# A hybrid RWKV-7 and pooling layer on one core: the stream's low weight parts on GpSimd, earlier loads for the output projection, no root in the key's norm, and a reordered tail

## The chip, the core and the metric

The kernel runs on one core of a Trainium2 chip. A core has a matrix engine (TensorE, PE in the profile, with PEld for its weight loads), three engines for elementwise work (VectorE = DVE, ScalarE = ACT, GpSimd = POOL), a queue engine (SyncE = SP) and DMA queues that the engines issue to. Each engine works through its own instructions in order, and waits where an instruction needs what another engine or a DMA has not delivered. The metric is the time of one execution in microseconds (us).

## What is computed

One layer for 512 tokens of width 2048. The essential lines of the reference:

```python
h = rms_norm(x, norm_g[i])
z = jnp.einsum('btd,dn->btn', h, w_in[i])
...
kk = (k * k_k[i]).astype(f32).reshape(B, T, N_HEADS, HEAD_SIZE)
kk = kk / jnp.maximum(jnp.linalg.norm(kk, axis=-1, keepdims=True), KK_EPS)
k = k * (1.0 + (a - 1.0) * k_a[i])
...
y = wkv7_scan(rh, wh, kh, vh, kk, ah)
y = head_group_norm(y, ln_w[i], ln_b[i])
...
y_mix = jnp.concatenate([y_rwkv, y_pool], axis=-1)
x = x + jnp.einsum('btc,cd->btd', y_mix, w_out[i])
gate = jax.nn.sigmoid(jnp.einsum('btd,de->bte', x, w_pg[i]) + b_pg[i])
x = x + gate * jnp.einsum('btq,qd->btd', p[i], w_ple[i])
...
return rms_norm(x, final_g)
```

z is cut into the key, receptance, value and gate of 16 heads of 64 (k, r, v, g) and into the inputs and gates of a pooling branch. `wkv7_scan` is a recurrence over the tokens, with a 64x64 state per head that each token decays, corrects along kk and adds to.

## The kernel before

All large products are made in three matmuls per tile (`mm3`): each operand is split into a high part in the matrix engine's rounded format and a low part, the rest; high·high, high·low and low·high are summed. A weight chunk is fetched and split by `wsplit` (L127): SP loads it into `raw`, ScalarE casts it to `whi` (L132), VectorE subtracts to `wlo` (L133). Activations are split the same way by `split` (L137, L138).

The program has these stages.

1. The input norm, transposes and small parameters, to about 40 us. `prm` holds the parameter vectors, one column per 128 channels (`pc`), and `dprm` the columns derived from them (`dp`).
2. The **stream**, to 746 us. TensorE's order is written out (`keep_in_program_order` while `pin` is set). A generator `stream()` makes the projections: for each of 8 head pairs j the units k, r, v and g; 16 units of the pooling branch (b) spread among them; and at the end four embed units (e) that compute p @ W_ple, store the result `ple` to DRAM (`pled`), and use two PSUM tiles in turn (`psA`). `pump(n)` lets the stream issue n matmuls. `chunk` (L174) takes the next weight chunk and fetches up to two ahead; raw, whi and wlo have four buffers each.
   Among the stream's matmuls stand the steps of the recurrence. The 512 tokens are cut into chunks of 64, and `recur` makes for each a chain of three **hops**: `py` (TensorE) to `zs` (VectorE, L753); `pu` to `uv` (ScalarE, L761); `ps` to the new state `sbd` (VectorE, L772), from which GpSimd makes the decayed `s0p` (L779) for the next chunk. Behind each hop stand stream matmuls (`pump(HC1)` and its like), so that TensorE has work while the hop runs. In the same time VectorE carries out the next head pair's `invert`: 31 steps of two small instructions each (L624, L628), placed three steps at a time behind a hop's VectorE instruction.
   Between two head pairs stand `prepare_key`, `norm_key` and `scale_key` (L521 to L541): the square of k·k_k, its sum over a head on TensorE (`pss`), the root on ScalarE (L535), a maximum on VectorE (L536), the reciprocal (L540) and the product kk. The maximum is kept as `late[0]`: `gather` issues its two transposes y (L701), from which TensorE makes `pq`, only behind it, and `scale_key` behind the second of them.
3. The output projection (`acc_o`), to 935 us, in four blocks of 512 columns. The layer's input to it lies in DRAM (`yd`); 16 loads `yin` (L890, three buffers) are issued on ScalarE's queue and split into `yhi` and `ylo`, in the order 8 to 13, 0 to 7, 14, 15.
4. The gate projection (`acc_g`), to 1112.7 us, in four blocks; the last one finishes one tile of 128 tokens after the other, the last of these in two halves (`acc_h`).
5. The **tail**. `gate` (L987) makes tanh of the gate, the sum with the residual and its square with a running sum (`ssq`); in the last block GpSimd multiplies by the final gain gB into `x3` (L1007). `norm` (L1011) makes one over the root of the mean: for the first three token tiles by a bit trick and three Newton steps on VectorE (`rsqrt`, L141), for the last by ScalarE's Sqrt and a reciprocal. Then four pieces of 512 columns are scaled and written out by SP (L1034).

What sets the order: inside the stream the matrix engine's is fixed by hand; on the other engines a scheduler places each instruction by priority, unless `issue_after` ties it behind another.

Of the kernel before, what the change touches and what calls it, by code (L numbers as in the profile page):

```python
# [9 lines left out]
F32 = mybir.dt.float32  # L10
# [24 lines left out]
def trunk_kernel(ctx: ExitStack, tc: tile.TileContext, x, p, norm_g, w_in, mu, w0, w_up, a0, a_up,  # L35
# [79 lines left out]
    dprm = cst.tile([P, 25 + 8 * 8], F32, name="dprm")  # L115

    def pc(n_, i):
        return prm[:, col[n_] + i:col[n_] + i + 1]
# [1 line left out]
    def dp(o, i):  # L120
        return dprm[:, o + i:o + i + 1]
# [2 lines left out]
    hlo = hp.tile([P, KT, T], F32R, name="hlo", tag="alo")  # L124


    def wsplit(src, kt, n, nm):  # L127
        raw = wp.tile([P, kt, n], F32, name=f"raw_{nm}", tag="raw")
        nc.sync.dma_start(out=raw, in_=src)
        hi = wp.tile([P, kt, n], F32R, name=f"whi_{nm}", tag="whi")  # L130
        lo = wp.tile([P, kt, n], F32R, name=f"wlo_{nm}", tag="wlo")
        nc.scalar.copy(hi, raw)  # L132
        nc.vector.tensor_tensor(lo, raw, hi.bitcast(F32), ALU.subtract)  # L133
        return hi, lo

    def split(hi, lo, src):
        nc.scalar.copy(hi, src)  # L137
        nc.vector.tensor_tensor(lo, src, hi.bitcast(F32), ALU.subtract)  # L138
# [176 lines left out]
    def derived(o, n_, cnt, m_, a_):  # L315
        nc.vector.tensor_scalar(dprm[:, o:o + cnt], prm[:, col[n_]:col[n_] + cnt], m_, a_, ALU.mult, ALU.add)
# [113 lines left out]
    def embed_unit(ec):  # L430
        ws = [chunk(f"e{ec}_{k}", 0) for k in range(2)]
        phi, plo = phl
        for tt in range(NT):
            ts_ = slice(tt * P, (tt + 1) * P)
            pq = psA.tile([P, EC], F32, name=f"pple{ec}_{tt}", tag="acc")
            for k in range(2):
                wh, wl = ws[k]
                mm(pq, phi[:, k, ts_], wh[:, 0, :], start=k == 0, stop=False)
                mm(pq, phi[:, k, ts_], wl[:, 0, :], start=False, stop=False)
                mm(pq, plo[:, k, ts_], wh[:, 0, :], start=False, stop=k == 1)  # L440
                if k == 0:
                    yield 3
            t_ = pp.tile([P, EC], F32, name=f"ple{ec}_{tt}", tag=("u", "sw")[tt % 2])
            nc.scalar.copy(t_, pq)
            nc.scalar.dma_start(out=pled[ts_, ec * EC:(ec + 1) * EC], in_=t_)
            yield 3
# [83 lines left out]
    def norm_key(j):  # L530
        kk, kqh, kql = kks[j]
        ps = psM.tile([P, T], F32, name=f"pss{j}", tag="m")
        mm(ps, blk, kqh, start=True, stop=False)
        mm(ps, blk, kql, start=False, stop=True)
        nc.scalar.activation(kk, ps, AF.Sqrt)  # L535
        late[0] = nc.vector.tensor_scalar(kk, kk, 1e-12, None, ALU.max)  # L536

    def scale_key(j):
        k_, kk = need("k", j), kks[j][0]
# [5 lines left out]
    def prepare(j):  # L545
# [332 lines left out]
    s2a.close()  # L878
    psB = ctx.enter_context(tc.tile_pool(name="psB", bufs=3, space=PSUM))
    lp = ctx.enter_context(tc.tile_pool(name="lp", bufs=1))  # L880
    pump(10 ** 6)
    pin[0] = False
    sy = ctx.enter_context(ExitStack())
    ymp = sy.enter_context(tc.tile_pool(name="ymp", bufs=1))
    yhi = ymp.tile([P, KT, T], F32R, name="yhi")
    ylo = ymp.tile([P, KT, T], F32R, name="ylo")
    order = [8, 9, 10, 11, 12, 13, 0, 1, 2, 3, 4, 5, 6, 7, 14, 15]
    for k in order:
        t_ = ymp.tile([P, T], F32, name=f"yin{k}", tag="yin", bufs=3)
        nc.scalar.dma_start(out=t_, in_=yd[k])  # L890
        split(yhi[:, k, :], ylo[:, k, :], t_)


    x2hi = hp.tile([P, KT, T], F32R, name="x2hi", tag="ahi")
# [1 line left out]
    x2d = dram.tile([T, D], F32, name="x2d", bufs=1)  # L896
    KEEP = 8
    TP = 40
    AS = (3,)
    last = [None]  # L900
    nacc = [0]

    def acc_tile(nm):
# [71 lines left out]
    with tc.tile_pool(name="fp", bufs=2) as fp, tc.tile_pool(name="kp_", bufs=1) as kp_:  # L975
# [5 lines left out]
        def vectors(ec):  # L981
# [4 lines left out]
            nc.scalar.dma_start(out=gB, in_=final_g[es].unsqueeze(0).to_broadcast([P, EC]))  # L986
            return bB, gB  # L987

        def gate(acc, ec, tt, cs, part):
# [9 lines left out]
            nc.vector.tensor_tensor(gt, acc, bB[:, lc], ALU.add)  # L999
            nc.scalar.activation(gt, gt, AF.Tanh, scale=0.5)  # L1000
            if part > LAST:
                tc.keep_in_program_order(nc.scalar.activation(warm, epsr, AF.Sqrt))
            nc.vector.scalar_tensor_tensor(gt, gt, 1.0, pl_[:, lc], ALU.add, ALU.mult)  # L1003
            nc.vector.scalar_tensor_tensor(gt, gt, 0.5, x2_[:, lc], ALU.mult, ALU.add)  # L1004
            nc.scalar.activation(x2_[:, lc], gt, AF.Square, accum_out=ssq[tt][:, part:part + 1])  # L1005
            if part <= LAST:
                (nc.gpsimd if ec == LAST else nc.vector).tensor_tensor(x3[tt][:, cs], gt, gB[:, lc], ALU.mult)  # L1007
            return gt

        def norm(tt, parts):  # L1010
            rows = slice(tt * P, (tt + 1) * P)  # L1011
            rs = fp.tile([P, 1], F32, name=f"frs{tt}", tag="frs")
            nc.vector.tensor_reduce(rs, ssq[tt][:, 0:parts], mybir.AxisListType.X, ALU.add)
            nc.vector.tensor_scalar(rs, rs, 1.0 / D, 1e-6, ALU.mult, ALU.add)
            if tt < NT - 1:
                fr = fp.tile([P, 1], F32, name=f"fr{tt}", tag="fr")
                ft = fp.tile([P, 1], F32, name=f"ft{tt}", tag="ft")
                rsqrt(fr, rs, ft)
                rs = fr
            else:  # L1020
                nc.scalar.activation(rs, rs, AF.Sqrt)
                nc.vector.reciprocal(rs, rs)
            for pc_ in range(D // EC):
                ps_ = slice(pc_ * EC, (pc_ + 1) * EC)
                if tt == NT - 1 and pc_ == LAST:
                    hs = slice(pc_ * EC, pc_ * EC + EC // 2)
                    nc.scalar.activation(x3[tt][:, hs], x3[tt][:, hs], AF.Copy, scale=rs)
                    nc.vector.scalar_tensor_tensor(x3[tt][:, hs.stop:D], last[0], rs, vec[1][:, EC // 2:EC],
                                                   ALU.mult, ALU.mult)
                elif pc_ in ((1,) if tt == NT - 1 else AS):  # L1030
                    nc.scalar.activation(x3[tt][:, ps_], x3[tt][:, ps_], AF.Copy, scale=rs)
# [22 lines left out]
        for tt in range(NT):  # L1054
            fetch(ec, tt)
        acc = proj(w_pg, x2hi, x2lo, ec, "g", keep=kept)
        for tt in range(NT):
            ts_ = slice(tt * P, (tt + 1) * P)
            hw = EC // len(acc[tt])
            for h, a_ in enumerate(acc[tt]):  # L1060
                hc = slice(h * hw, h * hw + hw)
                for k in range(KT - KEEP, KT):
                    wh, wl = kept[k]
                    mm3(a_, x2hi[:, k, ts_], x2lo[:, k, ts_], wh[:, 0, hc], wl[:, 0, hc], False, k == KT - 1)
                with tc.high_priority(offset=TP * tt):
                    last[0] = gate(a_, ec, tt, slice(ec * EC + hc.start, ec * EC + hc.stop), ec + h)
            with tc.high_priority(offset=TP * tt):
                norm(tt, LAST + len(acc[tt]))


_INS = ["x", "p", "norm_g", "w_in", "mu", "w0", "w_up", "a0", "a_up", "k_k", "k_a", "r_k", "ln_w", "ln_b",
# [19 lines left out]
```

## Time and profile before

| | us |
|---|---|
| three runs | 1126.79, 1126.81, 1129.08; median 1126.81 |
| profiled execution | 1126.0 |
| its span on the core | 1124.3 |

The span lies 1.7 us under the execution's own time. The busy time of the engines by stage (windows view; columns: from and to, length, then busy time and number of instructions of PE, PEld, DVE, ACT, POOL, then the granted clock, the DMA share and GB/s):

```profile
40.00:160.00 120.00, 119.91 (x685) 98.51 (x684) 85.49 (x201) 55.41 (x102) 4.13 (x9) 1.00 0.38 105
160.00:720.00 560.00, 546.01 (x3471) 439.44 (x3470) 420.38 (x1273) 244.16 (x513) 53.41 (x106) 1.00 0.34 92
720.00:746.40 26.40, 25.37 (x109) 19.39 (x107) 9.37 (x19) 14.90 (x25) 0.00 (x0) 1.00 0.75 239
746.40:935.00 188.60, 182.30 (x816) 150.53 (x816) 70.21 (x107) 55.92 (x94) 0.00 (x0) 0.98 0.48 161
935.00:1112.70 177.70, 177.69 (x835) 148.20 (x833) 87.34 (x157) 60.10 (x113) 3.88 (x3) 1.00 0.49 157
1112.70:1124.30 11.60, 0.00 (x0) 0.00 (x0) 5.75 (x20) 4.75 (x11) 0.73 (x1) 0.68 0.51 181
```

TensorE works for 546.0 of 560 us of the stream's main part; a busy matmul is pipelined, so this is not a measure of its peak. Between 720 and 746.4 lie the embed units, and the last row is the tail, in which TensorE has nothing left to do.

### The profile page before, as it was taken

The numbers are of one execution on the slowest core, as the hardware profiler recorded it, in microseconds if no ns is written. First come the engines' busy times: TensorE is split into PE (matmuls) and PEld (weight loads), VectorE is DVE, ScalarE is ACT, GpSimd is POOL, SyncE is SP. The second block draws the span as 40 slices with busy tenths as digits, with TensorE's granted clock in tenths as the row PEclk, the third lists the DMA queues.
The fourth block names the chain that finished last, engine by engine and source line by source line (L and its number), as shares of the span: only waits on it lengthen the run. The fifth ranks groups of instructions, "written<-read, shape, count | busy, mean of one in ns | idle before, by whom it ended". The sixth has DMA issues, their size and how long they took to land. (4 is left out here: it accounts for less than half of the span.)

```text
span 1124.3 us, 17316 instructions
## 1 busy us (share of the span) xinstructions
PE 1080.0 (96%) x6090; PEld 881.1 (78%) x6090; DVE 708.0 (63%) x1853; ACT 465.5 (41%) x928; POOL 71.6 (6%) x184
## 2 busy tenths in 40 slices
PE   5999999999999999999999999979999999999995
PEld 4888887777877877868778777758888888888885
DVE  7677868778579688786885956525323424345366
ACT  7553545335336245353353443444222222233243
POOL 2100010110010000200101001000000000000001
PEclk9999999999999999999999999989999999999998
DMA  7433332332433333333234332477434437355344
GB/s 227 122 94 97 101 103 68 106 90 77 118 83 95 99 85 92 98 85 97 73 99 117 87 112 73 135 250 260 165 100 164 143 118 233 108 189 155 128 131 150
DMA packets 178485, 138.56 MB, mean 123 GB/s; under 512 B 34677, under 2 KB 139742, under 8 KB 178398
## 3 DMA queue, kind: packets, MB, share of 16 engines
q1 hardware_dynamic: 157694, 103.89, 31.5%
q10 hardware_dynamic: 20704, 33.56, 9.3%
q8 instruction: 48, 0.79, 0.3%
q14 instruction: 39, 0.32, 0.1%
HBM read 118.02 MB, written 18.87 MB: 122 GB/s over the span
## 5 line engine op out<-in xcount | busy, mean ns | idle before, releaser
L133 DVE TENSOR_TENSOR wlo_g<-raw_g,whi_g 128x512 fp32r<-128x512 f32 x88 | 59.5, 683 | 84.7 <-ACT whi_g L132 82.6
L133 DVE TENSOR_TENSOR wlo_o<-raw_o,whi_o 128x512 fp32r<-128x512 f32 x64 | 43.9, 690 | 105.7 <-ACT whi_o L132 105.7
L156 PE MATMUL zb<-hhi,whi_b 128*128 128x512 f32 x256 | 108.0, 422 | 0.0
L156 PE MATMUL acc_o<-whi_o,yhi 128*128 128x512 f32 x256 | 101.2, 395 | 6.3 <-ACT yhi L137 6.3
L156 PE MATMUL acc_o<-whi_o,ylo 128*128 128x512 f32 x256 | 101.1, 395 | 0.0
L156 PE MATMUL acc_o<-wlo_o,yhi 128*128 128x512 f32 x256 | 100.7, 393 | 0.0
L156 PE MATMUL zb<-hhi,wlo_b 128*128 128x512 f32 x256 | 100.6, 393 | 0.0
L132 ACT CAST whi_g<-raw_g 128x512 fp32r<-128x512 f32 x88 | 54.3, 620 | 111.8 <-PE acc_g L156 71.7
L156 PE MATMUL zb<-hlo,whi_b 128*128 128x512 f32 x256 | 100.0, 390 | 0.0
L156 PE MATMUL acc_g<-whi_g,x2hi 128*128 128x512 f32 (+1 forms) x224 | 86.7, 387 | 0.0
L156 PE MATMUL acc_g<-wlo_g,x2hi 128*128 128x512 f32 (+1 forms) x224 | 86.4, 386 | 0.0
L156 PE MATMUL acc_g<-whi_g,x2lo 128*128 128x512 f32 x224 | 86.0, 385 | 0.0
L132 ACT CAST whi_o<-raw_o 128x512 fp32r<-128x512 f32 x64 | 39.9, 623 | 100.3 <-PE acc_o L156 95.8
L779 POOL TENSOR_SCALAR s0p<-sbd,pw 64x64 f32<-64x64 f32 x96 | 49.5, 516 | 343.2 <-DVE sbd L772 261.2
L132 ACT CAST whi_b<-raw_b 128x512 fp32r<-128x512 f32 x64 | 39.7, 620 | 73.0 <-PE zv L156 30.9
L133 DVE TENSOR_TENSOR wlo_b<-raw_b,whi_b 128x512 fp32r<-128x512 f32 x64 | 43.9, 686 | 35.5 <-ACT whi_b L132 32.9
L156 PEld LDWEIGHTS acc_o<-whi_o,yhi 128*128 128x128 f32 x256 | 48.7, 190 | 16.6 <-issue 6.7
L156 PEld LDWEIGHTS zb<-hhi,wlo_b 128*128 128x128 f32 x256 | 48.0, 188 | 11.2
L156 PEld LDWEIGHTS acc_o<-wlo_o,yhi 128*128 128x128 f32 x256 | 48.8, 191 | 10.1
L156 PEld LDWEIGHTS acc_o<-whi_o,ylo 128*128 128x128 f32 x256 | 48.6, 190 | 10.2 <-DVE ylo L138 0.2
L628 DVE TENSOR_TENSOR xw<-xw,tm 128x60 f32<-128x60 f32 (+24 forms) x248 | 51.9, 209 | 6.8
L156 PEld LDWEIGHTS zb<-hhi,whi_b 128*128 128x128 f32 x256 | 48.3, 189 | 8.5
(288 smaller groups left out, 2556.5 us busy)
## 6 DMA issues: line engine op xcount, KB each, us to landing
raw_b<-in_w_in_dram SPq DMA_DIRECT2D x64, 256.0 KB
raw_o<-in_w_out_dram SPq DMA_DIRECT2D x64, 256.0 KB
raw_g<-in_w_pg_dram SPq DMA_DIRECT2D x64, 256.0 KB
raw_k<-in_w_in_dram SPq DMA_DIRECT2D x32, 256.0 KB
raw_r<-in_w_in_dram SPq DMA_DIRECT2D x32, 256.0 KB
raw_v<-in_w_in_dram SPq DMA_DIRECT2D x32, 256.0 KB
raw_g<-in_w_in_dram SPq DMA_DIRECT2D x32, 256.0 KB
n<-nd SPq DMA_DIRECT2D x16, 256.0 KB
```

Source lines behind the costliest of these rows:

```text
L132: nc.scalar.copy(hi, raw)
L133: nc.vector.tensor_tensor(lo, raw, hi.bitcast(F32), ALU.subtract)
L156: i = nc.tensor.matmul(*a, **k)
L628: nc.vector.tensor_tensor(xw[:, 0:n_, s + 1:32], xw[:, 0:n_, s + 1:32], tm[:, 0:n_, 0:w_], ALU.add)
L779: nc.gpsimd.tensor_scalar(s0p[hc, :], nxt[hc, hc], pcn[hc], None, ALU.mult)
```

## The change

1. `chunk` hands GpSimd to `wsplit` as the engine of the low part. All low parts of the stream, 200 of 128x512 and 8 of 128x256, go from VectorE to GpSimd; those of the output and gate projections stay.
2. The first four `yin` loads are issued on SP's queue, and are written ahead of the last `pump`, which runs the rest of the stream; the other twelve stay on ScalarE's.
3. `norm_key` drops the root. VectorE takes the maximum (of 1e-24) from PSUM, so kk becomes k·k_k over the square of its norm, and the second factor, which stood as −kk in `ar`, becomes −k·k_k with a derived column `dp(89)`.
4. The embed units' PSUM tiles come from psA and psM in turn.
5. In the tail the multiplication by gB in the last block goes into the scaling (one VectorE instruction: gate · root · gain). All token tiles use ScalarE's Sqrt and a reciprocal. The loads of ScalarE's function tables for Sqrt and Tanh are brought on by dummy calls behind the last use of the other function. The last half's square goes to VectorE, and the scaling pieces of the last two token tiles are reordered.

```diff
-    def wsplit(src, kt, n, nm):
+    def wsplit(src, kt, n, nm, low=None):
...
-        nc.vector.tensor_tensor(lo, raw, hi.bitcast(F32), ALU.subtract)
+        (low or nc.vector).tensor_tensor(lo, raw, hi.bitcast(F32), ALU.subtract)
...
-                ready[n_, c_] = wsplit(src, kt, w_, f"{n_}_{c_}")
+                ready[n_, c_] = wsplit(src, kt, w_, f"{n_}_{c_}", nc.gpsimd)
...
+    derived(89, "k_k", 8, -1.0, 0.0)
...
-            pq = psA.tile([P, EC], F32, name=f"pple{ec}_{tt}", tag="acc")
+            pq = (psA, psM)[tt % 2].tile([P, EC], F32, name=f"pple{ec}_{tt}", tag=("acc", "m")[tt % 2])
...
-        nc.scalar.activation(kk, ps, AF.Sqrt)
-        late[0] = nc.vector.tensor_scalar(kk, kk, 1e-12, None, ALU.max)
+        late[0] = nc.vector.tensor_scalar(kk, ps, 1e-24, None, ALU.max)
...
-        nc.vector.scalar_tensor_tensor(ar[:, :, 1:3, :], k4, -1.0, pw4[:, :, :, 0:C], ALU.mult, ALU.mult)
+        nc.vector.scalar_tensor_tensor(ar[:, :, 1:3, :], k_.rearrange("p (q c t) -> p q c t", c=2, t=C), dp(89, j),
+                                       pw4[:, :, :, 0:C], ALU.mult, ALU.mult)
...
-    pump(10 ** 6)
-    pin[0] = False
...
-    for k in order:
+
+    def load_y(k, queue):
         t_ = ymp.tile([P, T], F32, name=f"yin{k}", tag="yin", bufs=3)
-        nc.scalar.dma_start(out=t_, in_=yd[k])
+        queue.dma_start(out=t_, in_=yd[k])
         split(yhi[:, k, :], ylo[:, k, :], t_)
+
+    for k in order[:4]:
+        load_y(k, nc.sync)
+    pump(10 ** 6)
+    pin[0] = False
+    for k in order[4:]:
+        load_y(k, nc.scalar)
...
-            nc.scalar.activation(gt, gt, AF.Tanh, scale=0.5)
+            th = nc.scalar.activation(gt, gt, AF.Tanh, scale=0.5)
+            if sq[0] is not None:
+                behind(th, sq[0])
+            if ec == LAST and (tt < NT - 1 or part > LAST):
+                with tc.issue_after(th.ins):
+                    nc.scalar.activation(warm, epsr, AF.Sqrt)
...
             if part > LAST:
+                nc.vector.scalar_tensor_tensor(x2_[:, lc], gt, 1.0, gt, ALU.mult, ALU.mult,
+                                               accum_out=ssq[tt][:, part:part + 1])
+            else:
+                nc.scalar.activation(x2_[:, lc], gt, AF.Square, accum_out=ssq[tt][:, part:part + 1])
+            if ec < LAST:
+                nc.vector.tensor_tensor(x3[tt][:, cs], gt, gB[:, lc], ALU.mult)
...
+            sq[0] = nc.scalar.activation(rs, rs, AF.Sqrt)
             if tt < NT - 1:
-                fr = fp.tile([P, 1], F32, name=f"fr{tt}", tag="fr")
-                ft = fp.tile([P, 1], F32, name=f"ft{tt}", tag="ft")
-                rsqrt(fr, rs, ft)
...
+                with tc.issue_after(sq[0].ins):
+                    nc.scalar.activation(warm, epsr, AF.Tanh)
+            nc.vector.reciprocal(rs, rs)
...
+                if pc_ == LAST:
...
+                        nc.vector.scalar_tensor_tensor(x3[tt][:, ps_.start + o_:ps_.start + o_ + w_], g_, rs,
+                                                       vec[1][:, o_:o_ + w_], ALU.mult, ALU.mult)
...
+                elif pc_ in ((1, 2) if tt == NT - 1 else (1,)):
```

How the instructions stand now, at three places. First GpSimd's queue in the middle of the stream, where only the s0p rows stood before. The names are those of the kernel (wlo, raw and whi of a k or r unit; s0p of a recurrence chunk), and what a row waits for follows it:

```order
L781 TENSOR_SCALAR s0p_1_4729<-sbd_566,pw_3362 64x64 [waits DVE_49]
L781 TENSOR_SCALAR s0p_1_4729<-sbd_566,pw_3362 64x64 [waits DVE_49,Pool_49]
L133 TENSOR_TENSOR wlo_r_0_2564<-raw_r_0_2561,whi_r_0_2563 128x512 [waits PE_49,DMAHW5_49,Activation_49,Pool_49]
L133 TENSOR_TENSOR wlo_r_1_2631<-raw_r_1_2628,whi_r_1_2630 128x512 [waits DMAHW6_49,PE_49,Activation_49]
L781 TENSOR_SCALAR s0p_2_4790<-sbd_567,pw_3362 64x64 [waits DVE_49]
L781 TENSOR_SCALAR s0p_2_4790<-sbd_567,pw_3362 64x64 [waits DVE_49,Pool_49]
L133 TENSOR_TENSOR wlo_r_2_2637<-raw_r_2_2634,whi_r_2_2636 128x512 [waits PE_49,DMAHW3_49,Activation_49,Pool_49]
L133 TENSOR_TENSOR wlo_r_3_2672<-raw_r_3_2669,whi_r_3_2671 128x512 [waits DMAHW6_49,PE_49,Activation_49]
L781 TENSOR_SCALAR s0p_3_4864<-sbd_566,pw_3362 64x64 [waits DVE_49]
L781 TENSOR_SCALAR s0p_3_4864<-sbd_566,pw_3362 64x64 [waits DVE_49,Pool_49]
```

Two s0p, one for each head, now stand in turn with two low parts.

Second VectorE between two head pairs, from the maximum (kk) on; wlo are low parts, sw and u belong to the pooling branch, yo to the recurrence's output. Before:

```order
L536 TENSOR_SCALAR kk_5873<-kk_5873 128x512 [waits Activation_49]
L133 TENSOR_TENSOR wlo_g_3_3292<-raw_g_3_3289,whi_g_3_3291 128x512 [waits DMAHW1_49,PE_49,Activation_49]
L404 TENSOR_TENSOR sw_1_5965<-u_5963 128x511 [waits Activation_49]
L405 COPY sw_1_5965<-u_5963 128x1
L827 TENSOR_TENSOR yo_5984<-yo_5984,bv_4629 128x512 [waits Activation_49]
L404 TENSOR_TENSOR sw_2_5968<-sw_1_5965 128x510 [waits DVE_49]
L405 COPY sw_2_5968<-sw_1_5965 128x2
L828 TENSOR_TENSOR yo_5984<-yo_5984,sg_4700 128x512 [waits DVE_49]
L133 TENSOR_TENSOR wlo_k_0_3298<-raw_k_0_3295,whi_k_0_3297 128x512 [waits DMAHW5_49,PE_49,Activation_49]
L407 TENSOR_TENSOR sw_2_5968<-sw_2_5968,rc_505 128x4 [waits DVE_49]
L701 STREAM_TRANSPOSE y_6004<-x_5773 32x256 [waits DMAHW2_49]
L408 SCALAR_TENSOR_TENSOR u_5963<-sw_2_5968,u_5963 128x512 [waits DVE_49]
```

and with the change:

```order
L537 TENSOR_SCALAR kk_5868<-pss_5944 128x512 [waits PE_49]
L703 STREAM_TRANSPOSE y_5998<-x_5768 32x256 [waits DMAHW2_49]
L703 STREAM_TRANSPOSE y_5998<-x_5768 32x256 [waits DMAHW0_49]
L541 RECIPROCAL kk_5868<-kk_5868 128x512 [waits DVE_49]
L405 TENSOR_TENSOR sw_1_5959<-u_5957 128x511 [waits Activation_49]
L406 COPY sw_1_5959<-u_5957 128x1
L829 TENSOR_TENSOR yo_5978<-yo_5978,bv_4625 128x512 [waits Activation_49]
```

Before, the second transpose y and the reciprocal follow on these rows. Now both y stand right behind the maximum, which reads pss itself, and the reciprocal right behind them.

Third ScalarE where the stream ends and the output projection begins; ple and pled are the embed results and their stores, yin and yhi the loaded and cast input of the projection, whi_o the weights' high parts (whi_o_8 and whi_o_9 stood further up before, among the ple rows). Before:

```order
L444 COPY ple_3_8078<-pple_3_8071 128x512 [waits DMAHW0_49,PE_49]
L445 DMA pled<-ple_2_8068 128x512 [waits Activation_49]
L445 DMA pled<-ple_3_8078 128x512 [waits Activation_49]
L890 DMA yin_8086<-yd 128x512 [waits Pool_49]
L890 DMA yin_8090<-yd 128x512 [waits DMAHW7_49]
L890 DMA yin_8094<-yd 128x512
L132 CAST whi_o_10_8195<-raw_o_10_8193 128x512 [waits DVE_49]
L137 CAST yhi<-yin_8086 128x512 [waits DMAHW6_49]
L137 CAST yhi<-yin_8090 128x512 [waits DMAHW7_49]
L132 CAST whi_o_11_8213<-raw_o_11_8211 128x512 [waits DVE_49]
L137 CAST yhi<-yin_8094 128x512 [waits DMAHW0_49]
```

and with the change:

```order
L445 COPY ple_3_8092<-pple_3_8085 128x512 [waits DMAHW7_49,PE_49]
L446 DMA pled<-ple_2_8082 128x512 [waits Activation_49]
L137 CAST yhi<-yin_7929 128x512 [waits DMAHW1_49]
L137 CAST yhi<-yin_7933 128x512 [waits DMAHW3_49]
L446 DMA pled<-ple_3_8092 128x512 [waits Activation_49]
L137 CAST yhi<-yin_7937 128x512 [waits DMAHW4_49]
L891 DMA yin_8095<-yd 128x512 [waits DMAHW0_49,DVE_49]
L132 CAST whi_o_8_8152<-raw_o_8_8150 128x512 [waits Pool_49]
L891 DMA yin_8099<-yd 128x512 [waits DVE_49]
L137 CAST yhi<-yin_7941 128x512 [waits DMAHW7_49]
L137 CAST yhi<-yin_8095 128x512 [waits DMAHW0_49]
L132 CAST whi_o_9_8170<-raw_o_9_8168 128x512 [waits Pool_49]
```

The casts yhi no longer stand behind loads issued on the same queue, and the casts of whi_o_8 and whi_o_9 stand behind three and five of them.

More of the change, by code (lines that the diff above doesn't have):

```diff
@@ L898, in trunk_kernel @@
     TP = 40
-    AS = (3,)
-    last = [None]
     nacc = [0]
@@ L1012, in norm, with root @@
+            if ec < LAST:
+                nc.vector.tensor_tensor(x3[tt][:, cs], gt, gB[:, lc], ALU.mult)
+            return gt, th, lead_
+        def root(tt, parts, meanwhile=None):
             rs = fp.tile([P, 1], F32, name=f"frs{tt}", tag="frs")
             nc.vector.tensor_reduce(rs, ssq[tt][:, 0:parts], mybir.AxisListType.X, ALU.add)
-            nc.vector.tensor_scalar(rs, rs, 1.0 / D, 1e-6, ALU.mult, ALU.add)
-            if tt < NT - 1:
-                fr = fp.tile([P, 1], F32, name=f"fr{tt}", tag="fr")
-                ft = fp.tile([P, 1], F32, name=f"ft{tt}", tag="ft")
-                rsqrt(fr, rs, ft)
[L1019 to L1022, printed above, removed]
@@ L1023, in norm @@
-            for pc_ in range(D // EC):
-                ps_ = slice(pc_ * EC, (pc_ + 1) * EC)
[L1025 to L1030, printed above, removed]
+            ms = nc.vector.tensor_scalar(rs, rs, 1.0 / D, 1e-6, ALU.mult, ALU.add)
@@ L1065, in trunk_kernel @@
                 with tc.high_priority(offset=TP * tt):
-                    last[0] = gate(a_, ec, tt, slice(ec * EC + hc.start, ec * EC + hc.stop), ec + h)
-            with tc.high_priority(offset=TP * tt):
-                norm(tt, LAST + len(acc[tt]))
+                    g_, th_, lead_ = gate(a_, ec, tt, slice(ec * EC + hc.start, ec * EC + hc.stop), ec + h)
+                gts.append(g_)
+                if tt == NT - 1 and h == 1:
+                    rs_, gts_ = rest
+                    with tc.high_priority(offset=TP * tt), tc.issue_after(th_.ins):
+                        scaled(tt - 1, rs_, gts_, (1,))
+                    with tc.high_priority(offset=TP * tt), tc.issue_after(lead_.ins):
+                        rs = root(tt, LAST + 2, lambda: scaled(tt - 1, rs_, gts_, (LAST,)))
+            with tc.high_priority(offset=TP * tt):
+                if tt < NT - 1:
+                    rs = root(tt, LAST + 1)
+                    scaled(tt, rs, gts, (0, 2) if tt == NT - 2 else range(LAST + 1))
+                    rest = rs, gts
+                else:
+                    scaled(tt, rs, gts, (0, 1, LAST, 2))
 _INS = ["x", "p", "norm_g", "w_in", "mu", "w0", "w_up", "a0", "a_up", "k_k", "k_a", "r_k", "ln_w", "ln_b",
```

30 lines of the change are left out of this document (20 added, 10 removed).

## The prediction

> **What bounds the kernel now.** I read the page first (busy time of each engine), then the list of what TensorE waited for, then the stretches where it waited. The page's busy rows:
>
> ```profile
> span 1124.3 us, 17316 instructions
> PE 1080.0 (96%) x6090; PEld 881.1 (78%) x6090; DVE 708.0 (63%) x1853; ACT 465.5 (41%) x928; POOL 71.6 (6%) x184
> ```
>
> TensorE is busy for 96% of the span, and the change leaves its 6090 matmuls as they are. So there are 44 us in which it stands still, plus the time it runs at a lower clock, and nothing else to win. VectorE is at 63% and GpSimd at 6%, so a move of work from the one to the other looks free, but it is worth only what TensorE waits for VectorE. The waits of TensorE (line, releaser: us in total, times, longest):
>
> ```profile
> PE acc_o L156 <- ACT yhi L137: 6.3, 1, 6.3
> PE py L156 <- DVE sbd L772: 5.2, 8, 1.1
> PE pq L156 <- DVE y L701: 3.1, 2, 1.9
> PE pu L156 <- DVE zs L753: 1.0, 2, 0.7
> PE pple L156 <- ACT ple L444: 0.9, 1, 0.9
> PE pp L156 <- ACT uv L658: 0.9, 1, 0.9
> PE pu L156 <- ACT x L719: 0.9, 1, 0.9
> PE pmv L156 <- ACT bkn L667: 0.9, 1, 0.9
> PE pss L156 <- ACT bkn L667: 0.8, 1, 0.8
> ```
>
> No wait for a low part (wlo) is in it: the subtractions themselves are early enough. What VectorE's load costs shows only where it is late with something else: sbd, y and zs, 5.2 + 3.1 + 1.0 = **9.3 us**. ScalarE's share within the stream is 0.9 + 0.9 + 0.9 + 0.8 = 3.5 us. The largest single stop, 6.3 us, stands between the stream and the output projection. The windows view (length, then busy time of PE, PEld, DVE, ACT, POOL, then the clock) shows the stretches:
>
> ```profile
> 480.00:560.00 80.00, 76.44 (x491) 61.56 (x490) 62.08 (x188) 35.98 (x74) 6.88 (x15) 1.00 0.32 85
> 752.00:758.00 6.00, 5.29 (x13) 4.12 (x14) 3.52 (x6) 3.44 (x6) 0.00 (x0) 0.50 0.64 201
> 759.00:800.00 41.00, 41.00 (x186) 33.88 (x185) 19.38 (x30) 15.52 (x26) 0.00 (x0) 1.00 0.63 211
> ```
>
> In 80 us of the stream VectorE is busy for 62 and GpSimd for 7. After the stop of 6.3 us the clock stands at 0.50: 13 matmuls in 5.29 us, while 186 took 41.00 later (0.22 each). Those 13 lost 5.29 − 13 × 0.22 = 2.4 us, and the crossing into this place costs 6.3 + 2.4 = **8.7 us** in all.
>
> **The change part by part. (a) Low parts on GpSimd.** 200 subtractions of 128x512 and 8 of 128x256 leave VectorE. The nearest rows for both engines:
>
> ```profile
> L133 DVE TENSOR_TENSOR wlo_k<-raw_k,whi_k 128x512 fp32r<-128x512 f32 x32 | 22.2, 696 | 22.5 <-ACT whi_k L132 22.3
> L1007 POOL TENSOR_TENSOR x<-gt,gB x4: 726/1292/1296, 1099.1 to 1112.9; 128x512 f32<-128x512 f32 x3, 128x256 f32<-128x256 f32 x1
> L779 POOL TENSOR_SCALAR s0p<-sbd,pw 64x64 f32<-64x64 f32 x96 | 49.5, 516 | 343.2 <-DVE sbd L772 261.2
> L628 DVE TENSOR_TENSOR xw<-xw,tm 128x60 f32<-128x60 f32 (+24 forms) x248 | 51.9, 209 | 6.8
> ```
>
> VectorE loses 200 × 0.69 + 8 × 0.42 = 141 us. GpSimd gains 200 × 1.29 + 8 × 0.73 = 264 us and stands at about 330 of 1124: as a sum there is room. Whether there is room at every place is another matter, for two reasons. First, s0p (the decayed state of the recurrence) now stands in one queue with the low parts: an s0p that becomes ready while one runs waits up to 1.29 us, two in a row 2.6 us; s0p is wanted by the next sbd, about one hop chain later (6.8 us of idle stood before it in the row below), so this by itself is covered. Second, the two engines get in each other's way:
>
> ```profile
> 1112.89 0.73 POOL L1007 TENSOR_TENSOR x<-gt,gB 128x256 f32<-128x256 f32 x1 [0.82 <-DVE frs L143]
> 1112.91 0.72 DVE L146 SCALAR_TENSOR_TENSOR ft<-fr,frs 128x1 f32<-128x1 f32 x1
> 1113.86 0.22 DVE L146 SCALAR_TENSOR_TENSOR ft<-fr,frs 128x1 f32<-128x1 f32 x1
> 694.63 0.67 DVE L404 TENSOR_TENSOR sw<-sw 128x510 f32<-128x510 f32 x1
> 694.80 0.81 POOL L779 TENSOR_SCALAR s0p<-sbd,pw 64x64 f32<-64x64 f32 x1 [6.84 <-DVE sbd L772]
> ```
>
> The same instruction of one element per lane (L146) takes 0.72 us beside the GpSimd multiply and 0.22 alone, and it ends 0.01 us after the multiply does. In the other direction an s0p that starts in the middle of a VectorE sum takes 0.81 instead of 0.52. So each holds up the other for as long as it runs. The Trainium skill, "SBUF — State Buffer", section "Who interferes with whom", says this as a rule: a VectorE instruction with two inputs in SBUF contends with a GpSimd instruction that reads SBUF, and the one that starts second "fully blocks". The trace agrees with it (0.72 against 0.22). By that rule taken alone the move gains nothing on VectorE's side wherever the two meet.
>
> The price of it: per head pair (about 82 us) stand some 25 low parts, 25 × 1.29 = 32 us of GpSimd, beside 248 / 8 × 2 × 0.21 = 13 us of the inverse's small two-input steps (L628 and its twin L624) and the large sums. As claims on the same time they fit: 62 − 18 = 44 us of VectorE and 7 + 32 = 39 of GpSimd in 80 us. But they don't fit by much, and not at each place. A chunk of the recurrence has three hops with 8 matmuls of the stream behind each, 8 × 0.22 = 1.8 us, of which the hop's own 0.28 and its issue leave 1.0 to 1.5. One block of at most 1.29 us is just covered there; two in a row are not. Best: nothing comes and the 9.3 us go (−9.3). Worst: 0.7 us over the cover in each of 4 chunks that run beside an inverse, in 7 head pairs, 4 × 7 × 0.7 = +20. I take **+2**, near the covered end, because the claims fit as a sum. Of what VectorE made late I count only y's 3.1 as gone, **−3** (how, under b); the sbd and zs waits I leave, since blocks now stand where its load stood.
>
> **(b) No root.** These leave ScalarE:
>
> ```profile
> L535 ACT ACT_TABLE_LOAD x8 | 10.3, 1283 | 0.1
> L363 ACT ACT_TABLE_LOAD x7 | 9.0, 1283 | 0.1
> L535 ACT ACTIVATE kk<-pss 128x512 f32<-128x512 f32 x8 | 4.8, 598 | 0.1
> ```
>
> That is 24 us of an engine at 41%; on the path stands only its 1.9 us per head pair between pss and the max. The max is the same VectorE count, now out of PSUM, and the 3.35 us reciprocal stays. The y transposes stand behind this max. In the late one
>
> ```profile
> 498.38 0.68 DVE L562 TENSOR_TENSOR ar<-sr,pw 128x512 f32<-128x512 f32 x1
> 500.37 0.42 DVE L536 TENSOR_SCALAR kk<-kk 128x512 f32<-128x512 f32 x1
> 504.64 0.42 DVE L701 STREAM_TRANSPOSE y<-x 32x256 f32<-32x256 f32 x1
> ```
>
> VectorE works without a break from the max at 500.37 to y at 504.64, nine instructions, of which two (low parts) leave VectorE and seven stand behind y in the new order. So y comes about 4 us sooner, more than the longest wait for it (1.9), and the 3.1 us counted above go, unless several blocks fall just there. What is late next is the reciprocal's result, 3.35 us later as before. Half of ScalarE's 3.5 us may go with it: **−1** (bounds 0 and −3.5).
>
> **(c) Loads of y.** Rows of the crossing now:
>
> ```profile
> 746.45 0.94 ACTq L445 DMA_DIRECT2D pled<-ple  x2
> 747.43 1.62 ACTq L890 DMA_DIRECT2D yin<-yd  x3
> 749.09 0.62 ACT L132 CAST whi_o<-raw_o 128x512 fp32r<-128x512 f32 x1 [2.06 <-issue]
> 751.99 0.62 ACT L137 CAST yhi<-yin 128x512 fp32r<-128x512 f32 x1 [2.28 <-DMA yin<-yd]
> 752.71 0.77 PE L156 MATMUL acc_o<-whi_o,yhi 128*128 128x512 f32 x1 [6.30 <-ACT yhi L137]
> 753.65 0.33 ACTq L890 DMA_DIRECT2D yin<-yd  x1
> 756.42 1.18 ACT L137 CAST yhi<-yin 128x512 fp32r<-128x512 f32 x2 [1.77 <-DMA yin<-yd]
> ```
>
> The three loads are issued behind the last ple store at 747.43, the first lands at 751.99. With SP issuing three of them in the embed part (SP's next work, raw_o_12, has to wait for a free buffer anyway), yhi 8, 9 and 10 can be cast at once. But the cast of whi_o_8, which was done early, now stands behind them on ScalarE. The walk: the last ple copy ends at 747.04; four casts follow, 4 × 0.62, and three DMA issues between them of 0.3 to 0.5 each: 750.4 to 751.0. TensorE stopped at 746.41, so the stop is 4.0 to 4.6 us instead of 6.3. Then each whi_o stands behind a y load of 2.8 us (753.65 to 756.42), while one weight chunk feeds 12 × 0.22 = 2.7 us of matmuls: 0 to 4 us of smaller stops follow, 1.5 taken. The half clock (2.4) was seen behind a stop of 6.3 and at no shorter one of the waits above, so it is likelier gone than not. Sum: 4.2 + 1.5 = 5.7 against 8.7, −3; as 4.2 is untried for the clock I take **−2** (bounds: −4.5, and +2 with all the smaller stops and the half clock). The Trainium skill, "TensorE: Matmul & The Clock Gate", Part 1, puts the fall behind one idle window of about 3.4 us of a free-running grid; the trace (0.50 after a stop of 6.3) agrees, and by it a stop of 4.2 us would hold a whole window in about one case of four, in which the 2.4 us are paid again.
>
> **(d) Embed.** Four accumulators instead of two in turn: of the 0.9 us wait and small delays, **−0.9** (0 to −1.5).
>
> **(e) Tail.**
>
> ```profile
> 1112.41 0.28 PE L156 MATMUL acc_h<-whk,x2lo 128*128 128x256 f32 x1
> 1114.00 0.42 DVE L999 TENSOR_TENSOR gt<-acc_h,bB 128x256 f32<-128x256 f32 x1
> 1114.94 1.28 ACT L1002 ACT_TABLE_LOAD   x1
> 1118.30 0.72 ACT L1031 ACTIVATE x<-x,frs 128x512 f32<-128x512 f32 x1 [0.23 <-DVE frs L1022]
> ```
>
> TensorE ends at 1112.69, but the add starts at 1114.00, behind the root's steps of the tile before and the blocked 0.72. Without them: add at 1113.2, tanh 1113.7, two steps of 0.42 to 1115.2, square on VectorE to 1115.65. On ScalarE the table load for the root follows a piece and a square, about 1115.2 to 1116.5, so it is late next: root 1116.6, reciprocal, first scaling at 1117.0 instead of 1118.30: **−1.3** (0 to −2).
>
> **The sum.** −1.3 −2 −0.9 −1 −3 +2 = −6.2 against the profiled execution of 1126.0 (span 1124.3 and 1.7 around it): 1119.8. That execution lies 0.8 under the median, so 1120.6; I say **1121**.
>
> **The rivals.**
> *Blocks decide (slower).* One mechanism: a low part on GpSimd stops VectorE's small steps of the inverse, and through its queue the hop behind them, beyond the fillers' cover. It decides if a block comes in more than about half of the chunks beside an inverse. For it: 0.72 against 0.22, and 39 us of GpSimd beside 44 of VectorE in 80. Against it: the fillers' 1.8 us, and no wait for wlo now. Price +10 to +20 in place of +2, beside the other terms' −8.2: 1129 to 1139. Chance 0.23; the near half lies below 1133.
> *What is won is given back.* whi_o behind y costs 4 us and the clock falls again (c: +2 in place of −2), and blocks of +4: −1.3 + 2 − 0.9 − 1 − 3 + 4 = −0.2, 1126.6. Within 0.2% of before, which is 2.3 us and about what a measurement of this kernel can tell from no change. Chance 0.15.
> *VectorE was the cause of all its waits.* The whole 9.3 and 3.5 us go, no blocks show, crossing −4.5, tail −2, embed −1.5: 20.8 at most, of which two thirds, 13.9: 1113. Chance 0.10.
>
> **How the numbers follow.** My forecast (1116 to 1124) holds 0.52. Faster by over 0.2%: 0.52 + 0.10 = 0.62; within 0.15; slower 0.23. The range leaves out half of the blocks' case (0.11) and what lies under 1111 (0.06): **1111 to 1133**.
>
> **What would show it.** (a): mean of wlo on GpSimd near 1.29 (over 1.5: blocked by VectorE); mean of L624 and L628 near 0.21 (over 0.3: blocked by GpSimd); the sum of PE's waits for sbd, zs and px under 9.3. (b) no wait of pq for y. (c) the stop before acc_o 4.0 to 4.5 us, released by whi_o, and a clock of 1.00 behind it. (d) no wait of pple for ple. (e) from the last matmul to the first scaling 4.3 us instead of 5.6. Wrong it would be by waits of py, pu or px for VectorE of over 15 us, or a clock of 0.50 at 751.

## The result, and the profile after

The change makes the kernel **slower**: 1158.2 us median (1157.57 to 1159.94, four runs) against 1127.3 (1126.79 to 1129.08, four runs), a ratio of 1.0269 with an interval of 1.0253 to 1.0284. The forecast was 1121, and the range (1111 to 1133) ends 25 us below the result. The profiled execution took 1159.94 us, its span is 1158.2.

Where the 33.9 us of span lie, by the first and the last matmul of each kind in the two traces:

| stage | before, us | after, us | difference |
|---|---|---|---|
| start to the first embed matmul | 721.7 | 752.7 | +31.0 |
| embed matmuls | 24.7 | 24.1 | −0.6 |
| stop before the output projection | 6.3 | 7.0 | +0.7 |
| output projection | 182.8 | 186.9 | +4.1 |
| gate projection, to the end of acc_h | 177.2 | 177.1 | −0.1 |
| end of the last matmul to the end of the last scaling | 6.9 | 5.7 | −1.2 |

Nearly all of it is the stream. There TensorE stands still for 48.5 us instead of 25.4, so 23 of the 31 us are longer waits; the other 8 are longer busy time of the same matmuls (704.2 us instead of 696.3), which no run takes apart. The page's busy rows after the change, with the same columns as before:

```profile
span 1158.2 us, 17356 instructions
PE 1089.6 (94%) x6090; PEld 880.2 (76%) x6090; DVE 681.9 (59%) x1627; ACT 449.5 (39%) x917; POOL 334.1 (29%) x388
```

GpSimd's 334 us are what was expected (330). VectorE's aren't: 141 us of low parts left it, and it is busy for only 26 us less. The waits of TensorE after the change:

```profile
PE py L156 <- DVE sbd L774: 18.7, 19, 1.8
PE acc_o L156 <- ACT whi_o L132: 8.9, 2, 7.0
PE pss L156 <- ACT bkn L669: 3.2, 4, 1.1
PE ps L156 <- ACT uv L763: 3.1, 5, 1.2
PE pu L156 <- DVE zs L755: 3.0, 6, 0.9
PE pu L156 <- ACT x L721: 2.5, 4, 1.2
```

The wait for sbd went from 5.2 us in 8 places to 18.7 in 19; zs from 1.0 to 3.0, uv at ps from 0.3 to 3.1. The wait of pq for y (3.1) is gone. With 21.7 us for sbd and zs together, the forecast's own sign of being wrong (over 15 us of waits for VectorE) is met. The groups of the page that answer for it:

```profile
L630 DVE TENSOR_TENSOR xw<-xw,tm 128x60 f32<-128x60 f32 (+24 forms) x248 | 86.7, 350 | 7.5
L626 DVE TENSOR_TENSOR tm<-xw,n 128x60 f32<-128x60 f32 (+10 forms) x240 | 72.8, 303 | 7.2
L133 POOL TENSOR_TENSOR wlo_b<-raw_b,whi_b 128x512 fp32r<-128x512 f32 x64 | 83.8, 1309 | 107.3 <-ACT whi_b L132 96.7
L133 POOL TENSOR_TENSOR wlo_k<-raw_k,whi_k 128x512 fp32r<-128x512 f32 x32 | 44.7, 1399 | 69.3 <-ACT whi_k L132 41.4
```

The low parts take about what the row of before gave for them, 1309 ns for wlo_b and 1399 for wlo_k beside 1292. But the inverse's steps, of which nothing was changed, take 350 and 303 ns in the mean instead of 209 and 211. A stretch of the timeline shows how (start, duration; the lines of one wait, those between left out):

```profile
647.02 1.39 POOL L133 TENSOR_TENSOR wlo_b<-raw_b,whi_b 128x512 fp32r<-128x512 f32 x1 [1.80 <-ACT whi_b L132]
647.17 1.78 DVE L405 TENSOR_TENSOR sw<-sw 128x508 f32<-128x508 f32 x1
...
649.34 0.69 DVE L409 SCALAR_TENSOR_TENSOR u<-sw,u 128x512 f32<-128x512 f32 x1
...
650.63 0.29 DVE L774 SCALAR_TENSOR_TENSOR sbd<-ps,pw,s0p 64x64 f32<-64x64 f32 x1
...
650.98 0.49 PE L156 MATMUL py<-sbd,ar 128*128 128x128 f32 x2 [1.50 <-DVE sbd L774]
```

A low part starts on GpSimd at 647.02. The sum L405 that VectorE begins 0.15 us later takes 1.78 us instead of the 0.68 of before, so it ends 0.54 us after the low part. sbd itself reads PSUM and one SBUF tile and is as short as ever (0.29), but it stands behind the delayed instructions on VectorE, and TensorE waits 1.50 us for it.

### The profile page after: what moved, and what is told of

It is laid out like the page before. It is cut to its first block, busy times and chain, and to the rows that moved or that the text cites. A ratio compares the mean times of both kernels' runs of the same rounds, so it can differ in the third digit from the quotient of the medians.

```text
span 1158.2 us, 17356 instructions
## 1 busy us (share of the span) xinstructions
PE 1089.6 (94%) x6090; PEld 880.2 (76%) x6090; DVE 681.9 (59%) x1627; ACT 449.5 (39%) x917; POOL 334.1 (29%) x388
## 5 line engine op out<-in xcount | busy, mean ns | idle before, releaser
L133 POOL TENSOR_TENSOR wlo_b<-raw_b,whi_b 128x512 fp32r<-128x512 f32 x64 | 83.8, 1309 | 107.3 <-ACT whi_b L132 96.7
L630 DVE TENSOR_TENSOR xw<-xw,tm 128x60 f32<-128x60 f32 (+24 forms) x248 | 86.7, 350 | 7.5
L133 DVE TENSOR_TENSOR wlo_g<-raw_g,whi_g 128x512 fp32r<-128x512 f32 x56 | 38.1, 690 | 80.1 <-ACT whi_g L132 78.1
L626 DVE TENSOR_TENSOR tm<-xw,n 128x60 f32<-128x60 f32 (+10 forms) x240 | 72.8, 303 | 7.2
L133 POOL TENSOR_TENSOR wlo_k<-raw_k,whi_k 128x512 fp32r<-128x512 f32 x32 | 44.7, 1399 | 69.3 <-ACT whi_k L132 41.4
L133 POOL TENSOR_TENSOR wlo_g<-raw_g,whi_g 128x512 fp32r<-128x512 f32 x32 | 43.8, 1370 | 66.3 <-ACT whi_g L132 59.9
L774 DVE SCALAR_TENSOR_TENSOR sbd<-ps,pw,s0p 64x64 f32<-64x64 f32 x96 | 27.1, 282 | 54.3 <-PE ps L156 52.4
```

Of the source, the lines that this page charges most:

```text
L133: (low or nc.vector).tensor_tensor(lo, raw, hi.bitcast(F32), ALU.subtract)
L626: nc.vector.tensor_tensor(tm[:, 0:n_, 0:w_], xin[:, 0:n_, s:s + 1].to_broadcast([P, n_, w_]), nb[s // 16][:, s % 16:s % 16 + 1, s + 1:32]. ...
L630: nc.vector.tensor_tensor(xw[:, 0:n_, s + 1:32], xw[:, 0:n_, s + 1:32], tm[:, 0:n_, 0:w_], ALU.add)
L774: lead[0] = nc.vector.scalar_tensor_tensor(nxt[hc, hc], pss[hc, hc], pcc[hc], s0p[hc, :], ALU.mult, ALU.add)
```

## The experiments

Two theories and a rival were to be told apart. **Access**: a GpSimd instruction that reads SBUF shuts out VectorE's instructions with two inputs there. **Queue**: s0p, and the release of the raw and whi buffers, stand behind low parts of 1.3 us in GpSimd's own queue. **Another part** of the change: the moved loads, the root, the embed units, the tail. Where a part of the kernel before is tried, its text is changed; where a part is undone, that of the changed one.

**e1: the changed kernel with the low parts back on VectorE.**

```diff
-                ready[n_, c_] = wsplit(src, kt, w_, f"{n_}_{c_}", nc.gpsimd)
+                ready[n_, c_] = wsplit(src, kt, w_, f"{n_}_{c_}")
```

> The changed kernel with the stream's low parts back on VectorE, all else as changed. If GpSimd's low parts are the cause (by the shared access or by its queue), the 31 us that the stream lost are gone: about 1126, between 1121 and 1129, with the y, embed, root and tail parts alone in it. If another part of the change costs the stream its time, it stays above 1140.

Measured: 1125.34 us, ratio 0.9982 (0.9973 to 0.9992). The loss is gone, so the other parts together don't cost the stream anything.

**e2: the kernel before with the low parts on GpSimd and nothing else.** The edit is the one of `wsplit` and `chunk` in the change.

> The kernel before with nothing but the stream's low parts moved to GpSimd. If they are the cause: 1153 to 1162, the sbd, zs and uv waits of TensorE as long as in the changed kernel, the inverse's steps at 300 to 350 ns instead of 210. If another part is the cause: 1120 to 1130.

Measured: 1158.44 us, ratio 1.0278 (1.0262 to 1.0293). One part carries the whole loss. VectorE is busy for 679.7 us in it, the sbd wait is 18.3.

**e3: the same, but GpSimd fills the low part with zeros and reads only 8 of its columns.**

```diff
-        (low or nc.vector).tensor_tensor(lo, raw, hi.bitcast(F32), ALU.subtract)
+        else:
+            zero = lo.rearrange("p k n -> p (k n)").bitcast(F32)
+            low.memset(zero, 0.0)
+            low.memset(zero, 0.0)
+            low.memset(zero[:, 0:192], 0.0)
+            low.tensor_tensor(lo[:, 0:1, 0:8], raw[:, 0:1, 0:8], hi[:, 0:1, 0:8].bitcast(F32), ALU.subtract)
```

> As the run before, but GpSimd fills the low part's tile with zeros (three memsets of together about 1.3 us, which read nothing) and computes only 8 of its columns: the low parts of the stream's weights are left out of the products. GpSimd's queue is as full as with the subtractions and VectorE as much relieved. If the access to SBUF for reading is what holds VectorE up: the inverse's steps are back at 210 ns and the time is 1120 to 1130. If it is the queue (s0p and the release of the raw and whi buffers standing behind 1.3 us instructions): 1150 to 1160, as with the subtractions.

Measured: 1116.49 us, ratio 0.9905 (0.9890 to 0.9920). VectorE's and GpSimd's rows in this run (busy, mean of one):

```profile
L635 DVE TENSOR_TENSOR xw<-xw,tm 128x60 f32<-128x60 f32 (+24 forms) x248 | 52.6, 212 | 7.4
L631 DVE TENSOR_TENSOR tm<-xw,n 128x60 f32<-128x60 f32 (+10 forms) x240 | 50.9, 212 | 7.2
...
L137 POOL MEMSET wlo_b<- 128x512 f32 x64 | 33.9, 530 | 77.4 <-PE zb L163 37.0 <-PE zv L163 32.4 <-PE zg L163 5.8
L138 POOL MEMSET wlo_b<- 128x512 f32 x64 | 33.7, 527 | 3.7
L139 POOL MEMSET wlo_b<- 128x192 f32 x64 | 16.9, 264 | 3.6
```

GpSimd is as busy with each chunk (530 + 527 + 264 = 1321 ns) and s0p stands behind it as before, yet the inverse's steps are back at 212 ns and the kernel is 42 us faster than e2, below even the expected 1120 to 1130. That speaks for access and against the queue: what costs is the reading. One difference is left: the memsets don't wait for the cast, so raw and whi come free sooner than in e2. The trace of e2 shows no price of that: in the stream TensorE waits for no whi and 0.6 us for a low part, and where it waits for ScalarE, none of the four instructions that ScalarE ran last had waited for GpSimd. VectorE's busy time gives the size: 589.5 us here, 679.7 in e2, so it was held up for 90 us, of which 42 reach TensorE.

**e4: the kernel before with the low parts computed by nobody** (the high part is multiplied in their place).

> The kernel before with the stream's low parts computed by nobody (the high part stands in their place in the product, so the low parts of the stream's weights are left out). VectorE is relieved of 141 us and GpSimd is given nothing: the most that any move of the low parts could win. If VectorE's load is what makes sbd, zs and y late: 9 us less, 1116 to 1120. If they are late for other reasons: 1123 to 1127.

Measured: 1114.36 us, ratio 0.9886 (0.9869 to 0.9902). It is the bound of what any move of these low parts can win: 13 us, more than the 9.3 that the list of waits gave.

**e8: the changed kernel with s0p on VectorE.**

```diff
-                        nc.gpsimd.tensor_scalar(s0p[hc, :], nxt[hc, hc], pcn[hc], None, ALU.mult)
+                        nc.vector.tensor_scalar(s0p[hc, :], nxt[hc, hc], pcn[hc], None, ALU.mult)
```

> The changed kernel with s0p moved from GpSimd to VectorE, so that no instruction of the recurrence stands in the low parts' queue any more. If what costs is that VectorE's own instructions are held up by GpSimd's reads: no gain, 1153 to 1162, sbd waits as long as in the changed kernel. If a good part is that s0p waits behind the low parts: 10 us or more less, 1148 or below.

Measured: 1167.14 us, ratio 1.0344 (1.0325 to 1.0363), even above the range for access, which fits that VectorE, the engine that is held up, has 96 instructions more; the zs wait rises to 9.2 us. Nothing is won by taking s0p out of the queue. The page of the changed kernel says the same of sbd, which needs s0p:

```profile
L774 DVE SCALAR_TENSOR_TENSOR sbd<-ps,pw,s0p 64x64 f32<-64x64 f32 x96 | 27.1, 282 | 54.3 <-PE ps L156 52.4
```

VectorE's idle time ahead of it is for ps; in no place did sbd wait for s0p.

**e9: every fourth low part on GpSimd.**

```diff
+                share[0] += 1
-                ready[n_, c_] = wsplit(src, kt, w_, f"{n_}_{c_}")
+                ready[n_, c_] = wsplit(src, kt, w_, f"{n_}_{c_}", nc.gpsimd if share[0] % 4 == 0 else None)
```

> The kernel before with every fourth low part of the stream on GpSimd (one of each unit's four), the rest on VectorE. If a single block is covered by the 8 matmuls behind a hop, as the prediction had it, and only two in a row are not: at or under before, 1122 to 1127, since VectorE is relieved of a quarter. If each block costs its share: a quarter of 42 less a quarter of 11, 1133 to 1137.

Measured: 1133.64 us, ratio 1.0048 (1.0031 to 1.0065). The prediction's cover of one block per hop doesn't hold: the loss is 6 us, and with the relief of a quarter (11 / 4) 9 us for 52 low parts, 0.17 us each; in e2 it was 42 / 208 = 0.20 each. The inverse's steps take 240 and 245 ns in the mean. At these two shares the price per low part is about the same, and a quarter is not free.

**e11: each low part in four instructions.**

```diff
+            for k in range(kt):
+                low.tensor_tensor(lo[:, k, :], raw[:, k, :], hi[:, k, :].bitcast(F32), ALU.subtract)
```

> The kernel before with the stream's low parts on GpSimd, each of the 192 of 128x512 with four weight blocks cut into four instructions of 128x128 (some 0.35 to 0.45 us each). If what a hop loses is the rest of one GpSimd instruction, a shorter one loses less: 1125 to 1140. If it is GpSimd's whole reading time, however it is cut: 1153 to 1165.

Measured: 1137.12 us, ratio 1.0090 (1.0073 to 1.0107). Half of the loss goes (1137 against e3's 1116: 21 us instead of 42), though GpSimd is busy for longer:

```profile
PE 1081.0 (95%) x6090; PEld 879.3 (77%) x6090; DVE 645.4 (57%) x1645; ACT 464.7 (41%) x928; POOL 444.5 (39%) x968
...
L137 POOL TENSOR_TENSOR wlo_b<-raw_b,whi_b 128x128 fp32r<-128x128 f32 x256 | 118.9, 496 | 77.9 <-ACT whi_b L132 66.4
```

VectorE is held up for 645.4 − 589.5 = 56 us instead of 90. So a part of the price is the length of a single hold, as the expectation said, but the move still loses.

**The crossing: e5, e6, e7.** In e1 the stop before the output projection was longer than before, 8.9 us. The queue's own waits in the changed kernel say why:

```profile
SPq L891 <- DMA raw_o<-in_w_out_dram: 4.7, 1, 4.7
SPq L891 <- PE pple L156: 3.3, 1, 3.3
```

The loads of y, although issued ahead of the last pump, wait for the last embed matmul: their buffers are cut from the memory of the recurrence's pool, and the embed matmuls still read a tile of that pool (hl). They go out at 776.83, when TensorE stops, and not earlier. That the memory is the reason is read from the kernel's text, and e6 tries it. e5 is e1 with these loads as they were before the change.

> The changed kernel with the low parts on VectorE and, besides, the loads of y as they were before (on ScalarE's queue, behind the last pump); the root, embed and tail parts stay. In the run with the new loads TensorE stood 8.9 us at the crossing instead of 6.3, and the output projection took 2.9 us longer. If the new loads cause that: 5 us less than that run, 1119 to 1122, the stop 6.3 us again. If it comes from the embed part: no change, 1124 to 1126.

Measured: 1123.92 us, ratio 0.9968 (0.9953 to 0.9984); 1.4 us under e1 and not 5, with intervals that overlap: most of the loss at the crossing stays, as the second expectation had it, though its range (from 1124) is missed by 0.1 us. The stop is 5.7 us, but 2.0 us of waits for whi_o follow, and the output projection takes 186.3 us from its first matmul to its last, beside 185.7 in e1 and 182.8 before. So moving the loads in the way of the change makes the stop longer and not the projection. In e5 the first cast of whi_o behind the stop (747.73) still stands behind a cast of y (747.20). Which part of the change moved it there isn't shown: it isn't the root (182.7 us in e10), and the embed and tail parts were not tried alone. In e6 the first three loads go into buffers of the pooling branch (`dh`, `dl`, `sgp`), with which the pooling branch is done by then:

```diff
+        tag = ("dh", "dl", "sgp")[n % 3]
+        shape = [P, T] if tag == "sgp" else [P, 2, T]
+        t_ = pp.tile(shape, F32, name=f"yin{k}", tag=tag, bufs=1)
...
+    for n in range(3):
+        load_y(n, nc.sync)
+    pump(10 ** 6)
```

> As the run before, but the first three loads of y go into buffers that the pooling branch has done with (not into memory that the embed matmuls still hold), on SP, ahead of the last pump; their casts stay behind it. If the memory was what made the new loads late: they land before the embed units end, TensorE stops for 3 to 4 us (four casts) and keeps its clock, 1114 to 1117. If the loads' time is not what counts: the stop stays above 6 us, 1119 to 1122.

Measured: 1119.25 us, ratio 0.9921 (0.9904 to 0.9938). The three loads now go out between 720.8 and 727.7 us, so the memory was what held them. The direction is as expected, the size is not: the stop is 4.3 us, and the clock still falls (0.56 in the two us from 748). The projection is back at 182.2 us. In e7 the first weight chunk is split ahead of the casts of y:

```diff
+    first = {k: wsplit(w_out[k * P:(k + 1) * P, 0:EC].unsqueeze(1), 1, EC, f"o0_{k}") for k in order[:1]}
...
-                wh, wl = wsplit(src, 1, EC, f"{nm}{ec}_{k}")
+                wh, wl = first.pop(k) if nm == "o" and k in first else wsplit(src, 1, EC, f"{nm}{ec}_{k}")
```

> As the run before, with the first weight chunk of the output projection split ahead of the casts of y, so that two casts stand between the last embed copy and the first matmul instead of four. If the order of ScalarE's casts is what is left of the stop: 1.3 us less, a stop of about 2 us, 1113 to 1116. If a DMA is: no change from that run.

Measured: 1116.17 us, ratio 0.9896 (0.9881 to 0.9911). The stop is 2.0 us, and the time is 3.1 us less than e6's, where 1.3 was expected:

```profile
742.83 0.59 ACT L445 COPY ple<-pple 128x512 f32<-128x512 f32 x1 [0.45 <-DMA pled<-ple]
743.31 0.62 ACT L132 CAST whi_o<-raw_o 128x512 fp32r<-128x512 f32 x1
...
743.83 1.66 ACT L137 CAST yhi<-yin 128x512 fp32r<-128x512 f32 x3
```

With the low parts on VectorE and the root, embed and tail parts of the change, this version beats both kernels: 11 us under the one before, 42 under the changed one.

**e10: the kernel before without the root.** The edit is that of `norm_key`, `ar` and `derived` in the change.

> The kernel before with nothing but the root of the key's norm left out (maximum from PSUM, minus k times k_k in ar). The prediction put y's 3.1 us on this part and on the low parts together, and 1 us on ScalarE's. If the order behind the maximum is what made y late: the two waits of pq for y are gone, 1123 to 1126. If VectorE's low parts were: they stay, 1126 to 1128.

Measured: 1126.57 us beside 1129.03 of before, measured along with it, ratio 0.9981 (0.9967 to 0.9995). No wait of pq for y is left, so the order behind the maximum is enough. But the same wait is also gone in e2, e3 and e4, which keep the root: relief of VectorE does it too. The two explanations of the expectation were not exclusive, and the time lies in the range of the other one (1126 to 1128).

## Why the prediction was wrong, step by step

- **What bounds the kernel**: right in kind, small in size. VectorE's load does make hops late; taking the low parts off it is worth 11 us (e3) to 13 (e4), where the wait list gave 9.3 and the forecast counted 3.
- **(a) The step that failed** is the price of the blocks, "+2, near the covered end, because the claims fit as a sum". The mechanism was seen, with its row (0.72 beside 0.22), and stood as the rival *blocks decide*; its worst case was +20. The runs show +42 (e2 against e3). Together with the −3 for y, the move was forecast at −1; e2 alone is 31 us slower than before. Two things in the working were wrong. The cover of 1.0 to 1.5 us per hop was taken as free, although TensorE already waited at eight sbd hops with up to 1.1 us: at those there was none left. Elsewhere some was, since 48 of the 90 us that VectorE was held up for never reached TensorE; but e9 and e2 show 0.17 and 0.20 us lost per low part. And the claims were added over 80 us, as if they met by chance; but sbd isn't held up itself (282 ns, as before); it is late because of whatever two-input instruction stands ahead of it on VectorE, and that one may be held for the length of a low part, 1.3 us. The count of 4 chunks in 7 head pairs at 0.7 us left out the blocks of the large sums, of which the timeline above shows one.
- **GpSimd's queue** ("by itself covered"): right as far as the runs tell: by e3 and e8, and no sbd waits for s0p.
- The forecast's own sentence on the Trainium skill ("SBUF — State Buffer", "Who interferes with whom") gave the sign: by that rule the move gains nothing where the two meet. e3 agrees with its other half too, that a GpSimd instruction which only writes doesn't contend with two-input instructions: 212 ns beside 350.
- **(b)** The wait for y went, 3.1 us, as said. Of ScalarE's 3.5 us only the 0.9 of pu for x is gone in e10, about the 1 that was taken; but the waits of pm for bk, 0.3 before, are 1.6 there. e10 is about 2 us faster than before, and not 4; its lists of waits give 3.1 + 0.9 − 1.3 = 2.7, and the embed units waited longer in its profiled execution (2.6 us for ple instead of 0.9), for a reason that no run shows.
- **(c)** failed as well: −2 was forecast, +4.8 measured at this place (0.7 in the stop and 4.1 in the output projection). The step that failed is that the loads are issued "in the embed part": they waited for the last embed matmul. The stop was put at 4.0 to 4.6 and was 7.0; where the loads do go out in the embed part (e6) it is 4.3, so the walk itself was right. The longer projection isn't the loads' doing, since e5 has it without them; its cause stays open. That whi_o stands behind the casts of y was seen rightly: 1.84 us of a second stop at 804.79, and by e7 it is worth 3 us.
- The clock did not stay up. Around the crossing of the changed kernel it fell twice, behind the stop of 7.0 us and again at 806 (below), where the forecast took the one fall of 2.4 us as likelier gone than not. Even behind e6's stop of 4.3 us, the size that was forecast, it fell.
- **(d)** −0.9 forecast, −0.6 in the changed kernel and −1.7 in e1, from the length of the embed stage in the traces; no run tried it alone.
- **(e)** −1.3 forecast, −1.2 measured. From the last matmul to the first scaling:

```profile
1147.56 0.28 PE L156 MATMUL acc_h<-whk,x2lo 128*128 128x256 f32 x1
1150.27 1.28 ACT L1018 ACT_TABLE_LOAD   x1
1152.19 1.33 ACT L1057 ACTIVATE x<-x,frs 128x512 f32<-128x512 f32 x2 [0.33 <-DVE frs L1042]
```

  The table load is what is late next, as the walk said, and 1152.19 − 1147.84 = 4.35 us stand beside the 4.3 foretold.

The rival that came true stood at 1129 to 1139 with a chance of 0.23, and the range took in half of it; its price was too small by half (+20 at most, +42 measured).

## What to carry to other kernels

An idle engine is no free place for work if it reads SBUF while VectorE, for whose results the matrix engine waits, works with two inputs there: price each such instruction by how long it holds VectorE's queue, not by the sum of busy times. Where TensorE already waits at a hop, there is no cover, and every delay counts from the first. A load that is written earlier starts earlier only if its buffer is free: look at what the buffer's memory held, and who reads it last.

## What the runs showed of the hardware

The clock fell behind shorter stops than expected. Windows of the run e7 (length, then busy time and number of PE and the other engines' instructions, then the clock) around its stop of 2.0 us, and of the changed kernel at two places where TensorE worked for about half of the time, one at the crossing and one in the stream:

```profile
742.00:744.00 2.00, 0.48 (x3) 0.04 (x1) 0.03 (x1) 1.55 (x4) 0.00 (x0) 1.00 0.89 316
744.00:746.00 2.00, 1.42 (x4) 0.97 (x5) 2.00 (x4) 1.49 (x3) 0.00 (x0) 0.87 0.48 165
746.00:748.00 2.00, 2.00 (x6) 1.52 (x6) 0.95 (x2) 0.62 (x1) 0.00 (x0) 0.50 0.79 203
```

```profile
802.00:804.00 2.00, 0.95 (x5) 0.45 (x3) 1.07 (x2) 0.34 (x1) 0.00 (x0) 1.00 0.52 158
804.00:806.00 2.00, 0.98 (x3) 0.62 (x4) 0.69 (x1) 0.66 (x2) 0.00 (x0) 0.96 0.40 145
806.00:808.00 2.00, 2.00 (x7) 1.52 (x6) 1.39 (x3) 2.00 (x4) 0.00 (x0) 0.50 0.55 150
```

```profile
106.00:108.00 2.00, 0.83 (x3) 0.30 (x2) 1.79 (x7) 2.00 (x4) 0.74 (x1) 1.00 0.00 0
108.00:110.00 2.00, 1.41 (x5) 1.18 (x6) 1.93 (x3) 1.85 (x4) 2.00 (x3) 0.88 0.07 20
110.00:112.00 2.00, 2.00 (x6) 1.51 (x6) 1.97 (x2) 0.00 (x0) 2.00 (x2) 0.50 0.38 111
```

In the first the clock is at 0.50 after a stop of only 2.0 us; in the second and the third, matmuls busy for 1.9 and 2.2 of 4 us were too few to keep it. At 110 us the kernel before has no such fall (1.00). A full idle stretch of 3.4 us, as the Trainium skill has it ("TensorE: Matmul & The Clock Gate", Part 1), is thus not needed here. What share of a stretch is needed, these runs don't tell.
